# Moving the last 24 modulation column tiles of a diffusion trunk step: from the weight ring to residual places and to the second feed-forward half-step

## The chip, the cores and the metric

The kernel runs on one core of one Trainium2 chip. A core has a matrix engine (TensorE, PE in the profile), a vector engine (VectorE, DVE), a scalar engine (ScalarE, ACT), a general-purpose engine (GpSimd, POOL), and a synchronisation engine (SyncE, SP) that here only issues DMAs. GpSimd issues DMAs too, from a queue of its own. The metric is the time of one execution on the device in microseconds (us). It is judged by the median of several runs.

## The reference

One layer of a diffusion trunk on 640 tokens (512 latent tokens and 128 context tokens) of width 1024, in float32. What matters for the change are the nine modulation vectors, which come from a product of a conditioning vector with a wide matrix, and the places in the layer where each of them is used:

```python
def adaln(cvec, w, b):
    m = jax.nn.silu(cvec) @ w + b
    return m.reshape(cvec.shape[0], N_MOD, D_MODEL)

def layer(x, mods, l, p, ctx):
    m = [mods[:, j][:, None, :] for j in range(N_MOD)]
    g = p['g_norm'][l]
    hh = rmsnorm(x, g[0]) * (1 + m[1]) + m[0]
    x = x + 0.5 * m[2] * swiglu(hh, p['ffn1_w1'][l], p['ffn1_w3'][l], p['ffn1_w2'][l])
    hh = rmsnorm(x, g[1]) * (1 + m[4]) + m[3]
    y, ctx_out = token_mixer(hh, p, l, ctx)
    x = x + m[5] * y
    hh = rmsnorm(x, g[2]) * (1 + m[7]) + m[6]
    x = x + 0.5 * m[8] * swiglu(hh, p['ffn2_w1'][l], p['ffn2_w3'][l], p['ffn2_w2'][l])
    return x, ctx_out
```

The token mixer has a matrix-memory branch (a chunkwise recurrence with a 256 x 256 state for each of four heads) and a differential-attention branch. Each branch has an output product (`w_br_m`, `w_br_d`) whose result is multiplied with a sigmoid gate; the sum of the two goes through `w_out`.

## The kernel before

Features lie on the 128 partitions, eight tiles of them (`KT`), and tokens on the free axis, in two halves of 320 (`HALF`). Products with float32 precision are three matmuls: the weight is split into a high and a low part (`wH`, `wL`; ScalarE copies the high part, VectorE subtracts it), and so is the activation (`hH`, `hL`).

The stages follow one another: the first half-step, the projections and the attention, the matrix-memory stage, the end of the attention branch (product with `w_brd`, evacuated by VectorE as `y1`), the memory branch (product with `w_brm`, evacuated as `ym` and split into `hH` and `hL`), the output product (`w_out`), and the second half-step. TensorE's instructions run in the order in which they are written. Most of the others are put in an order by a scheduler, which looks at their dependencies and an estimate of durations; each engine and each DMA queue then runs its list in order.

*Column tiles.* The modulation of the latent and context tokens needs, for `j` from 2 to 8, 56 tiles of 128 output columns. A tile is a DMA of 128 x 1024 float32 (512 KB, `raw_a<-in_w_ada_c`) and, on VectorE, two reductions of it with the two conditioning rows (`csil`). `Columns.place(n, csil, load, ahead)` says where the next `n` tiles have their buffers and starts to fetch `ahead` of them; `Columns.tile()` takes one: it issues its two reductions and then the next fetch. Behind the eighth tile of a `j` comes a small addition of the bias, and for some of them what uses it (`columns.then`): the scale of the third norm behind `j` = 7, the half gate `half_m[:, 1]` of the last residual addition behind `j` = 8. The first 32 tiles are done in the first half-step. The last 24, of `j` = 6, 7 and 8, are the subject.

*The weight ring.* `rawp` has two slots of 128 x 2048 float32, and all projection weights (`raw<-...`), the re-read attention output (`a_raw`) and the re-read memory output (`z_raw`) go through it, by SP's queue, in order. The last 24 tiles use it as well (`load_columns_raw`, by SP; the reductions write their elementwise product into the other half of the same slot, as bfloat16). Ten of them stand between the cells of the matrix-memory stage, three beside `mem[3].finish`, five beside the last units of the attention branch, and six beside the units of the memory branch, one for every two units.

*Fill.* Products are handed out in units (`Fill`): a granule is the weight of 256 output columns, and has four units of 24 matmuls (two column tiles, two token halves). `fill.slot` runs units between the cells of the matrix-memory stage, `fill.units(2)` and `fill.drain()` run the rest.

*The second half-step.* `HalfStep.run` calls `products` with 20 work items `i` (w1 for even `i`, w3 for odd). An item is seven products of half-size blocks, and for its weights VectorE splits sums of blocks (`ww`, `wC`, `wB`) and evacuates (`s`, `t`, `SO`). `between(i, at)` is called at two places of each item; `hs.at_vec` is the last evacuation on VectorE. The tiles of x (`x_pairs`, in the four places `k0` to `k3`) hold first the layer's input for the residual addition behind `w_out`, then take part in the sums of the activation (`operand_sums`), and are read again from DRAM (`x2_dram`) for the last residual addition. In the kernel before, this re-read is issued at `(0, 1)`.

Of the kernel before, what the change touches and what calls it, by code (L numbers as in the profile page):

```python
# [16 lines left out]
D = 1024  # L17
# [5 lines left out]
KT = D // 128  # L23
# [8 lines left out]
def tile_trunk(ctx: ExitStack, tc: tile.TileContext, a: dict):  # L32
    nc = tc.nc
# [98 lines left out]
    half_m = cp.tile([128, 2, KT, 2], F32, name="half_m")  # L132
# [8 lines left out]
    def half(hf):  # L141
        return slice(hf * HALF, (hf + 1) * HALF)
# [310 lines left out]
    class HalfStep(Winograd):  # L453
# [95 lines left out]
        def run_whole(self, x, gate, final, between, ahead):  # L549
# [47 lines left out]
            for j in range(1, 4):  # L597
                for f in range(2):
                    unit(G[-1], j, f, 1)

        def run(self, x, gate, final, ahead, after):


            def nothing(*args):
                pass

            n = self.n_plain
            down = [Whole(n, self.fetch_w2(0, n, j)) for j in range(4)]

            up = self.ops  # L610
            at = [[up[i] for i in (A11, S1, S2, A12)], [up[i] for i in (S3, S4, A22)], None]

            def fetch(q, i, eng=nc.sync):
                b0, b1 = ((0, n), *GROUPS)[q]
                eng.dma_start(out=at[q][i][:, :, : b1 - b0].bitcast(F32), in_=self.g_dram[i, :, :, b0:b1, :])

            work = self.up_work()
            work[-1][3] = lambda i: {A11: lambda: fetch(0, 0), S1: lambda: fetch(0, 1), S2: lambda: fetch(0, 2), A12: lambda: fetch(0, 3)}.get(i, nothing)()

            def between(i, at):  # L620
                if (i, at) == (0, 1):
                    with tc.issue_after(work[1][0].split_at):
                        after()

            self.products(work, between, down[:2], ahead)
            at[1] += [self.fp.tile([128, 2, 4, HALF], F32R, tag=tag, name="op") for tag in ("gA", "SO")] + at[0][:2]
            x = x()

            def down_done(q, j):
                def done(f, hf, p, u):  # L630
                    d = 2 * j + f
                    if u is not None:
                        p = self.add(p, u)
                    add_residual(x, p, d, hf, gate)
                    if q == 2:
                        final(d, hf)

                def used(i):
                    if q == 1 and j == 3 and i in moves:
                        fetch(2, moves[i], nc.gpsimd)  # L640

                return done, used

            last = [
                [Granule(b1 - b0, self.fetch_w2(b0, b1, j)), lambda i, q=q: at[q][i], *down_done(q, j)]
                for q, (b0, b1) in zip((1, 2), GROUPS) for j in range(4)
            ]
            at[2] = at[0][2:] + at[1][:5]

            moves = {A11: S2, S1: A12, S2: S3, A12: A22, S3: S4}  # L650
            for j in range(4):
                ahead = down[j + 2] if j < 2 else last[j - 2][0]
                loaded = ahead.load()
                with tc.issue_after(loaded):
                    for i in ((A11, S1), (S2, A12), (S3,), ())[j]:
                        fetch(1, i)
                if j < 3:
                    down[j + 1].split()
                else:
                    last[0][0].parts(self.fp)  # L660
                    last[0][0].sums()
                for hf in range(2):
                    for f in range(2):
                        p = acc_tile(self.psum)
                        for kh in range(2):
                            op = at[0][PLAIN_Q[kh, hf]]
                            for b in range(n):
                                w = [down[j].w(i, n * kh + b, f) for i in range(2)]
                                mm3(p, *w, op[:, 0, b], op[:, 1, b], kh + b == 0, kh == 1 and b == n - 1)
                        add_residual(x, p, 2 * j + f, hf, gate)  # L670
                    if (j, hf) == (3, 0):
                        for i in (A22, S4):
                            fetch(1, i, nc.gpsimd)

            def load_last(load=last[3][0].load):
                with tc.issue_after(load()):
                    for i in (A11, S1):
                        fetch(2, i)

            last[3][0].load = load_last  # L680
            self.products(last, nothing, prepared=True)


    csil_dram = dp.tile([2, D], F32, name="csil_dram")
# [45 lines left out]
    x_dram = dp.tile([128, KT, T], F32, name="x_dram")  # L730
    hh2 = []
    stats = []
    with ExitStack() as ph:
# [9 lines left out]
        hs = HalfStep(1, fp, ntmp, psum, a["w1a"], a["w3a"], a["w2a"], FB)  # L743
# [205 lines left out]
        for f, hf in ((0, 1), (1, 1), (0, 0), (1, 0)):  # L949
            p = acc_tile(psum)  # L950
# [3 lines left out]
        with tc.issue_after(end.ins), tc.issue_after(at_act.ins):  # L954
            third, fourth = hs.operand_sums(lambda r: x_all[:, 2 * r : 2 * r + 2, :])
# [5 lines left out]
        columns = Columns(56)  # L961
# [97 lines left out]
        x = Now()  # L1059
# [141 lines left out]
    fill = Fill()  # L1201
# [349 lines left out]
    def pair(tag, i, name):  # L1551
        return in_pools[tag].tile([128, 2, T], F32, tag=f"{tag}{i}", name=name)

    def pairs(tag, name):
        return [pair(tag, i, name) for i in range(4)]
# [138 lines left out]
    with tc.issue_after(box["normed"]):  # L1694
        third, fourth = G.operand_sums(lambda r: box["x"][1][:, 2 * r : 2 * r + 2, :])
# [73 lines left out]
    def aside(hd, qi, part):  # L1769
        if hd == 0:  # L1770
            for _ in range(ROWS.get((qi, part), 0)):
                next(rows, None)
        if part == 0:
            with written():
                fill.low()
        if part == 1 and hd == 1 and qi in (1, 2):
            gate_load(qi - 1)
        if part == 0 and hd == 1 and qi in (2, 3):
            gate_cols()
# [9 lines left out]
    for hd in range(8):  # L1789
        H = heads[hd]  # L1790
        odd = hd % 2
        for qi in range(5):
            n = UNITS[hd][qi]
# [24 lines left out]
        n = UNITS[hd][-1]  # L1818
# [187 lines left out]
    csil2 = ada_p.tile([128, 2, D], F32, name="csil")  # L2006
    dma(csil2, csil_dram.partition_broadcast(128))
    in_order[0] = False
    columns.place(24, csil2, load_columns_raw, 1)
    with written():  # L2010
        fill.units(2)
    for i in range(5):
# [50 lines left out]
    for i in range(5):  # L2063
        fill.one()
        mem[3].finish(i)
        if i > 1:
            columns.tile()
    for k in range(6):
        if k % 3 == 0:
            raw = load(rawp, [128, 3, T], zT_dram[:, k : k + 3, :], tag="raw", name="z_raw")  # L2070
        act(zH[:, k], raw[:, k % 3], AF.Copy)
        tt(vec, zL[:, k], raw[:, k % 3], zH[:, k].bitcast(F32), ALU.subtract)
    while fill.q:
        fill.units(2)
        if columns.n > 6:
            columns.tile()
    ml.close()
    mix.close()

# [1 line left out]
    tmp = ctx.enter_context(tc.tile_pool(name="tmp", bufs=1))  # L2081
    out = ExitStack()
    zp = out.enter_context(tc.tile_pool(name="yy", bufs=1))
    x_pairs = pairs("k", "x")
    x = [x_pairs[d // 2][:, d % 2, :] for d in range(KT)]
    with tc.tile_pool(name="gate", bufs=1) as gp:
        yH, yL = hh_tiles(zp)
        yHL = [(yH[:, k], yL[:, k]) for k in range(KT)]

        def m_evac(g):  # L2090
            def f(p, mt, hf):
                cs = half(hf)
                t = gp.tile([128, HALF], F32, tag="ym", name="ym", bufs=3)
                tt(vec, t, p, gate_of(gm_dram, g, mt, hf, pool=gp, tag="sig", bufs=2), ALU.mult)
                tt(vec, t, t, y1[g][:, mt, cs], ALU.add)
                d = 2 * g + mt
                act(yH[:, d, cs], t, AF.Copy)
                tt(vec, yL[:, d, cs], t, yH[:, d, cs].bitcast(F32), ALU.subtract)
            return f

        for g in range(4):
            fill.granule(a["w_brm"][g], feat_units(psum, m_evac(g), zHL))
        for g in range(4):
            nc.sync.dma_start(out=x_pairs[g], in_=x_dram[:, 2 * g : 2 * g + 2, :])
        while fill.q:
            fill.units(2)
            if columns.n:
                columns.tile()
    ada.close()
    fp = out.enter_context(tc.tile_pool(name="out", bufs=1))  # L2110
    class Halves:
        def __init__(self, lo, hi):
# [9 lines left out]
    raw = load_raw(a["w_out"][3])  # L2122
    t = [in_pools["q"].tile([128, 1024], F32R, tag=f"q{i}", name="wo") for i in range(4)]
# [8 lines left out]
    hs = HalfStep(2, None, tmp, psum, a["w1b"], a["w3b"], a["w2b"], GROUPS[0][0])  # L2132
    st = [Stats(x, hf, tmp) for hf in range(2)]
    x2_dram = dp.tile([128, KT, T], F32, name="x2_dram")
# [60 lines left out]
    third, fourth = hs.operand_sums(lambda r: x_pairs[r])  # L2195
    SO = hs.SO

    def after():
        fourth()
        for g in range(4):  # L2200
            nc.sync.dma_start(out=x_pairs[g], in_=x2_dram[:, 2 * g : 2 * g + 2, :])
        hs.store_g(SO, 0)

    hs.run(
        lambda: x, half_m[:, 1], lambda d, hf: nc.sync.dma_start(out=a["y"][:, d, half(hf)], in_=x[d][:, half(hf)]),
        third, after,
    )


# [126 lines left out]
```

## Time and profile before

| what | us |
|---|---|
| median of 3 runs | 1838.76 (1837.59 to 1839.71) |
| the profiled execution | 1840.36 |
| its span | 1838.6 |
| TensorE busy | 1799.5 |
| VectorE busy | 1317.2 |
| ScalarE busy | 867.7 |

The span is the time from the first to the last instruction of the profiled execution. Busy times are unions over the span, so the rest of TensorE's share is time in which it ran no matmul. A row of a timeline has the start, the duration, the engine, the line of the kernel, the operation, what it writes and reads with the shapes, and in brackets the idle time of the engine before it and what ended it. A row of the waits has the sum in us, the number and the longest. SPq and POOLq are the engines' DMA queues.

### The profile page before, as it was taken

What the parts mean: (1) busy time and instruction counts of PE and PEld (TensorE: products, weight loads), DVE (VectorE), ACT (ScalarE), POOL (GpSimd) and SP (SyncE); (2) the same over time, 40 slices, a digit from 0 to 9 for tenths busy, and PEclk for the clock granted to TensorE, in tenths of its full rate; (3) what the DMA queues carried; (4) which work ended last, traced back from release to release, by engine and by line L of the source; (5) the groups of instructions that cost most, each with busy time, mean ns of one, the idle gap of its engine ahead of it and who ended that gap; (6) DMA issues with size and microseconds to landing.
All of it is one profiled execution on the core that took longest, in us unless ns stands there. A gap on an engine that the chain in (4) does not pass through costs nothing.

```text
span 1838.6 us, 30679 instructions
## 1 busy us (share of the span) xinstructions
PE 1799.5 (98%) x12608; PEld 1761.4 (96%) x12608; DVE 1317.2 (72%) x2148; ACT 867.7 (47%) x1490; POOL 31.0 (2%) x55
## 2 busy tenths in 40 slices
PE   7999999999999999999999999999899999999999
PEld 5999999999999999999999999999899999999999
DVE  5898886577787757475585558876766878887575
ACT  4654454112655555454465555673235645554232
POOL 0000001110000000000000000000000000000000
PEclk8999999999999999999999999999999999999999
DMA  7354547975234322122222154574742345447872
GB/s 289 121 192 169 193 169 250 370 239 176 72 122 145 122 81 79 63 85 67 77 77 84 41 168 147 199 268 164 257 174 86 132 149 188 166 170 254 322 286 87
DMA packets 127709, 298.77 MB, mean 162 GB/s; under 512 B 9617, under 2 KB 90769, under 8 KB 114769
## 3 DMA queue, kind: packets, MB, share of 16 engines
q1 hardware_dynamic: 118306, 256.44, 40.1%
q0 software_dynamic: 9264, 40.37, 6.0%
q8 instruction: 99, 1.62, 0.4%
q14 instruction: 40, 0.33, 0.1%
HBM read 233.15 MB, written 63.63 MB: 161 GB/s over the span
## 4 chain that ended last, share of the span: by engine, by line
PE 84%; DVE 6%; DMA 5%; ACT 3%; issue 1%; SPq 0%; DVEq 0%; ACTq 0%
PE ps_f L75 45%; PE ps_p L75 16%; PE ps_t L75 11%; PE sc L75 3%; PE ps_o L75 2%; PE ps_n L75 2%; DMA ada<-csil_dram 2%; DVE ww L54 1%; PE ps_u L75 1%; PE ps_wT L78 1%; DMA raw_a<-in_w_ada_c 1%; PE ps_qkT L78 1%; DVE raw_a L716 1%; ACT wH L51 1%; PE ps_ss L75 1%
## 5 line engine op out<-in xcount | busy, mean ns | idle before, releaser
L75 PE MATMUL ps_f<-S,ww 128*128 128x320 f32 x2172 | 350.2, 310 | 5.8 <-DVE ww L54 4.2
L75 PEld LDWEIGHTS ps_f<-S,ww 128*128 128x128 f32 x2172 | 327.0, 189 | 8.5 <-DVE ww L54 6.9
L75 PE MATMUL ps_p<-hH,wH 128*128 128x320 f32 x672 | 213.4, 318 | 6.9 <-DVE y L54 6.2
L75 PE MATMUL ps_p<-hL,wH 128*128 128x320 f32 x672 | 208.2, 310 | 0.0
L75 PE MATMUL ps_p<-hH,wL 128*128 128x320 f32 x672 | 208.2, 310 | 0.0
L51 ACT ACTIVATE ww<-raw 128x2048 fp32r<-128x2048 f32 (+1 forms) x67 | 125.6, 1874 | 154.9 <-PE ps_f L75 87.6
L75 PE MATMUL ps_f<-hm,ww 128*128 128x320 f32 x1236 | 195.6, 311 | 2.5 <-DVE ww L54 2.5
L75 PEld LDWEIGHTS ps_f<-hm,ww 128*128 128x128 f32 x1236 | 185.8, 189 | 2.8 <-DVE ww L54 2.8
L75 PE MATMUL ps_t<-wH,hH 128*128 128x256 f32 x640 | 185.3, 289 | 0.9 <-DVE x L57 0.9
L75 PE MATMUL ps_t<-wH,hL 128*128 128x256 f32 x640 | 181.1, 283 | 0.9 <-DVE hL L54 0.9
L75 PE MATMUL ps_t<-wL,hH 128*128 128x256 f32 x640 | 180.9, 283 | 0.0
L54 DVE TENSOR_TENSOR ww<-raw,ww 128x2048 fp32r<-128x2048 f32 (+1 forms) x67 | 150.1, 2240 | 38.7 <-ACT ww L51 38.7
L75 PE MATMUL ps_f<-hm,wB 128*128 128x320 f32 x984 | 157.6, 309 | 0.0
L75 PEld LDWEIGHTS ps_f<-hm,wB 128*128 128x128 f32 x984 | 147.7, 188 | 0.0
L54 DVE TENSOR_TENSOR raw<-raw 128x1024 f32<-128x1024 f32 x159 | 137.6, 865 | 2.0
L75 PEld LDWEIGHTS ps_p<-hH,wH 128*128 128x128 f32 x672 | 126.9, 189 | 7.6 <-ACT wH L51 6.4
L75 PEld LDWEIGHTS ps_p<-hL,wH 128*128 128x128 f32 x672 | 126.9, 189 | 0.3
L75 PEld LDWEIGHTS ps_p<-hH,wL 128*128 128x128 f32 x672 | 126.7, 189 | 0.0
L54 DVE TENSOR_TENSOR wL<-raw,wH 128x2048 fp32r<-128x2048 f32 x43 | 98.3, 2286 | 35.6 <-ACT wH L51 35.6
L75 PEld LDWEIGHTS ps_t<-wH,hH 128*128 128x128 f32 x640 | 122.4, 191 | 1.5 <-ACT nsq L51 1.1
L75 PEld LDWEIGHTS ps_t<-wH,hL 128*128 128x128 f32 x640 | 122.4, 191 | 1.1 <-DVE hL L54 1.1
L75 PEld LDWEIGHTS ps_t<-wL,hH 128*128 128x128 f32 x640 | 122.5, 191 | 0.4
(303 smaller groups left out, 3353.7 us busy)
## 6 DMA issues: line engine op xcount, KB each, us to landing
g_dram<-g SPq DMA_DIRECT2D x44, 640.0 KB, 5.6
raw_a<-in_w_ada_c SPq DMA_DIRECT2D x24, 512.0 KB, 4.0
raw<-in_w1b SPq DMA_DIRECT2D x11, 1024.0 KB, 4.8
raw<-in_w3b SPq DMA_DIRECT2D x11, 1024.0 KB, 4.8
raw<-in_w1a SPq DMA_DIRECT2D x10, 1024.0 KB, 4.8
raw<-in_w3a SPq DMA_DIRECT2D x10, 1024.0 KB, 6.2
ada<-in_w_ada_c POOLq DMA_DIRECT2D x18, 512.0 KB, 5.0
hm<-g_dram POOLq DMA_DIRECT2D x7, 1280.0 KB, 10.5
```

The lines of the kernel that those rows point to most:

```text
L51: return placed(nc.scalar.activation(*args, **kw))
L54: return placed(eng.tensor_tensor(out=out, in0=in0, in1=in1, op=op))
L75: tc.keep_in_program_order(nc.tensor.matmul(*args, **kw))
L78: tc.keep_in_program_order(nc.tensor.transpose(*args, **kw))
L716: placed(vec.tensor_tensor_reduce(out=junk, in0=raw, in1=self.csil[:, v, :], op0=ALU.mult, op1=ALU.add, scale=1.0, scalar=0.0, accum_out=m ...
```

## The change

The 24 tiles are given other places in time and other buffers:

- ten stay in the matrix-memory stage, in the weight ring, as before;
- none is left in the attention branch's end (eight before);
- six stay beside the memory branch's units, but fetched by GpSimd's queue into one buffer of their own (place `k2`), with their product written to `k3` as float32. So only two of the four x loads stand at the beginning of this branch, and the other two follow behind the sixth tile;
- eight stand in the second half-step, at the odd items 3 to 17, with one buffer in `k2`, their product in `k3` and the two `csil` rows read again into `k0` and `k1` at `(1, 1)`. The re-read of x comes at `(18, 1)`, when those places are free again.

```diff
--- before.py
+++ after.py
@@ -598,7 +598,7 @@
                 for f in range(2):
                     unit(G[-1], j, f, 1)
 
-        def run(self, x, gate, final, ahead, after):
+        def run(self, x, gate, final, ahead, aside):
 
 
             def nothing(*args):
@@ -620,7 +620,9 @@
             def between(i, at):
                 if (i, at) == (0, 1):
                     with tc.issue_after(work[1][0].split_at):
-                        after()
+                        aside(i, at)
+                else:
+                    aside(i, at)
 
             self.products(work, between, down[:2], ahead)
             at[1] += [self.fp.tile([128, 2, 4, HALF], F32R, tag=tag, name="op") for tag in ("gA", "SO")] + at[0][:2]
@@ -2006,7 +2008,7 @@
     csil2 = ada_p.tile([128, 2, D], F32, name="csil")
     dma(csil2, csil_dram.partition_broadcast(128))
     in_order[0] = False
-    columns.place(24, csil2, load_columns_raw, 1)
+    columns.place(10, csil2, load_columns_raw, 1)
     with written():
         fill.units(2)
     for i in range(5):
@@ -2063,17 +2065,12 @@
     for i in range(5):
         fill.one()
         mem[3].finish(i)
-        if i > 1:
-            columns.tile()
     for k in range(6):
         if k % 3 == 0:
             raw = load(rawp, [128, 3, T], zT_dram[:, k : k + 3, :], tag="raw", name="z_raw")
         act(zH[:, k], raw[:, k % 3], AF.Copy)
         tt(vec, zL[:, k], raw[:, k % 3], zH[:, k].bitcast(F32), ALU.subtract)
-    while fill.q:
-        fill.units(2)
-        if columns.n > 6:
-            columns.tile()
+    fill.drain()
     ml.close()
     mix.close()
 
@@ -2081,8 +2078,15 @@
     tmp = ctx.enter_context(tc.tile_pool(name="tmp", bufs=1))
     out = ExitStack()
     zp = out.enter_context(tc.tile_pool(name="yy", bufs=1))
-    x_pairs = pairs("k", "x")
-    x = [x_pairs[d // 2][:, d % 2, :] for d in range(KT)]
+    x_pairs = [pair("k", i, "x") for i in range(2)]
+
+    def load_columns_pair(src):
+        raw = pair("k", 2, "raw_a").rearrange("p a t -> p (a t)")[:, :D]
+        nc.gpsimd.dma_start(out=raw, in_=src)
+        return raw, junk
+
+    junk = pair("k", 3, "junk").rearrange("p a t -> p (a t)")[:, :D]
+    columns.place(6, csil2, load_columns_pair, 1)
     with tc.tile_pool(name="gate", bufs=1) as gp:
         yH, yL = hh_tiles(zp)
         yHL = [(yH[:, k], yL[:, k]) for k in range(KT)]
@@ -2100,13 +2104,18 @@
 
         for g in range(4):
             fill.granule(a["w_brm"][g], feat_units(psum, m_evac(g), zHL))
-        for g in range(4):
+        for g in range(2):
             nc.sync.dma_start(out=x_pairs[g], in_=x_dram[:, 2 * g : 2 * g + 2, :])
         while fill.q:
             fill.units(2)
             if columns.n:
                 columns.tile()
+                if not columns.n:
+                    x_pairs += [pair("k", i, "x") for i in range(2, 4)]
+                    for g in range(2, 4):
+                        nc.sync.dma_start(out=x_pairs[g], in_=x_dram[:, 2 * g : 2 * g + 2, :])
     ada.close()
+    x = [x_pairs[d // 2][:, d % 2, :] for d in range(KT)]
     fp = out.enter_context(tc.tile_pool(name="out", bufs=1))
     class Halves:
         def __init__(self, lo, hi):
@@ -2195,15 +2204,36 @@
     third, fourth = hs.operand_sums(lambda r: x_pairs[r])
     SO = hs.SO
 
-    def after():
-        fourth()
-        for g in range(4):
-            nc.sync.dma_start(out=x_pairs[g], in_=x2_dram[:, 2 * g : 2 * g + 2, :])
-        hs.store_g(SO, 0)
+    places = []
+
+    def load_columns_pair(src):
+        raw = pair("k", 2, "raw_a").rearrange("p a t -> p (a t)")[:, :D]
+        nc.gpsimd.dma_start(out=raw, in_=src)
+        return raw, places[2]
+
+    def aside(i, at):
+        if (i, at) == (0, 1):
+            fourth()
+            hs.store_g(SO, 0)
+        elif (i, at) == (1, 1):
+            places.extend(pair("k", j, n).rearrange("p a t -> p (a t)")[:, :D] for j, n in ((0, "csil"), (1, "csil"), (3, "junk")))
+            for v in range(2):
+                nc.sync.dma_start(out=places[v], in_=csil_dram[v].partition_broadcast(128))
+            columns.place(8, Two(places[:2]), load_columns_pair, 1)
+        elif at and 3 <= i < 3 + 15 and i % 2 == 1:
+            columns.tile(hs.at_vec)
+        elif (i, at) == (18, 1):
+            x_pairs[:] = pairs("k", "x")
+            for g in range(4):
+                nc.sync.dma_start(out=x_pairs[g], in_=x2_dram[:, 2 * g : 2 * g + 2, :])
+
+    def residual_pairs():
+        x[:] = [x_pairs[d // 2][:, d % 2, :] for d in range(KT)]
+        return x
 
     hs.run(
-        lambda: x, half_m[:, 1], lambda d, hf: nc.sync.dma_start(out=a["y"][:, d, half(hf)], in_=x[d][:, half(hf)]),
-        third, after,
+        residual_pairs, half_m[:, 1], lambda d, hf: nc.sync.dma_start(out=a["y"][:, d, half(hf)], in_=x[d][:, half(hf)]),
+        third, aside,
     )
```

The order of the other engines moves with it. The first place is SP's queue at the end of the attention branch: `raw<-in_w_brd` and `raw<-in_w_brm` are the ring's weights of the two branches, `raw_a` the tiles, `x` the residual, `sig` the gates. Before:

```order
L97 DMA raw_a<-in_w_ada_c 128x1024
L97 DMA raw<-in_w_brd 128x2048
L97 DMA raw_a<-in_w_ada_c 128x1024 x4
L97 DMA raw<-in_w_brm 128x2048 x2
L2104 DMA x<-x_dram 128x1280 x4
L97 DMA raw_a<-in_w_ada_c 128x1024
L97 DMA sig<-gm_dram 128x1280 x2
```

And after:

```order
L97 DMA z_raw<-zT_dram 128x1920 x2
L97 DMA sig<-gd_dram 128x1280
L97 DMA raw<-in_w_brd 128x2048
L97 DMA raw<-in_w_brm 128x2048 x3
L2108 DMA x<-x_dram 128x1280 x2
L97 DMA sig<-gm_dram 128x1280 x2
L97 DMA raw<-in_w_brm 128x2048
```

The tiles are gone from this queue, and the memory branch's weights stand directly behind the attention branch's last one.

The second place is ScalarE at the end of the matrix-memory stage, behind one and the same evacuation `hs`. `aHL` is the high part of the attention output, `wv`, `Cn`, `num` and `hjunk` belong to the cells, `stage` evacuates a unit of a projection. Before:

```order
L51 ACTIVATE wv<-va,cols 128x258
L51 ACTIVATE Cn<-ps_u 128x258 x2
L51 ACTIVATE hjunk,hss<-hs 128x256 x4
L51 ACTIVATE stage<-ps_p 128x320
L51 ACTIVATE num<-ps_n_12691,cols 128x258
L51 ACTIVATE hjunk,hss<-hs 128x256
L51 ACTIVATE wv<-va,cols 128x258
L51 ACTIVATE rt<-rv 128x5
L51 ACTIVATE ry<-rt 128x5
L51 ACTIVATE num<-ps_n_12713,cols 128x258
L51 ACTIVATE hs<-num,den 128x256
L51 ACTIVATE wv<-va,cols 128x258
```

And after:

```order
L51 ACTIVATE aHL<-a_raw 128x640 x3
L51 ACTIVATE wv<-va,cols 128x258
L51 ACTIVATE hjunk,hss<-hs 128x256
L51 ACTIVATE Cn<-ps_u 128x258 x2
L51 ACTIVATE hjunk,hss<-hs 128x256
L51 ACTIVATE stage<-ps_p 128x320
L51 ACTIVATE hjunk,hss<-hs 128x256 x2
L51 ACTIVATE num<-ps_n_12689,cols 128x258
L51 ACTIVATE hjunk,hss<-hs 128x256
L51 ACTIVATE wv<-va,cols 128x258
L51 ACTIVATE aHL<-a_raw 128x640 x3
```

Before, the first `aHL` copies follow behind the last of these rows; after, three stand ahead of them and three more ahead of the next cells' `num`.

The third place is VectorE in the second half-step, around the low part of a weight block (`ww`) of an odd item. Before:

```order
L54 TENSOR_TENSOR s<-ps_f,u 128x320
L54 TENSOR_TENSOR ww<-raw,ww 128x2048
L54 TENSOR_TENSOR wC<-raw,wC 128x512
L54 TENSOR_TENSOR SO<-ps_f,s 128x320
L54 TENSOR_TENSOR wB<-raw,wB 128x1024
L54 TENSOR_TENSOR t<-ps_f,u 128x320
```

And after, at the third to the eighth tile (at the first two, `ww` and `wC` still stand ahead of `SO`):

```order
L54 TENSOR_TENSOR s<-ps_f,u 128x320
L54 TENSOR_TENSOR SO<-ps_f,s 128x320
L718 ISA junk,mod<-raw_a,csil 128x1024
L718 ISA mod 128x1
L54 TENSOR_TENSOR ww<-raw,ww 128x2048
L54 TENSOR_TENSOR wC<-raw,wC 128x512
L718 ISA junk,mod<-raw_a,csil 128x1024
L718 ISA mod 128x1
L54 TENSOR_TENSOR wB<-raw,wB 128x1024
L54 TENSOR_TENSOR t<-ps_f,u 128x320
```

`SO` and the tile's first reduction moved ahead of `ww`, and the second reduction ahead of `wB`.

## The prediction

> **What bounds the kernel now.** I read the page's shares of busy time and its chain first, since they say whether a stage is worth anything at all.
>
> ```profile
> PE 1799.5 (98%) x12608; PEld 1761.4 (96%) x12608; DVE 1317.2 (72%) x2148; ACT 867.7 (47%) x1490; POOL 31.0 (2%) x55
> PE 84%; DVE 6%; DMA 5%; ACT 3%; issue 1%; SPq 0%; DVEq 0%; ACTq 0%
> ```
>
> TensorE is busy 98% of the span, and its instructions are the same after the change. So only what TensorE loses between matmuls can be won, and every new wait of TensorE adds to the end. The second view is the busy time in stretches around the places that the change empties and fills (columns: window, PE, PEld, DVE, ACT, POOL busy, PE clock, DMA share, GB/s).
>
> ```profile
> 1270.00:1285.00 15.00, 13.92 (x95) 13.66 (x94) 7.59 (x14) 1.92 (x1) 0.00 (x0) 1.00 0.49 172
> 1285.00:1300.00 15.00, 9.71 (x67) 9.45 (x65) 10.36 (x17) 3.25 (x2) 0.00 (x0) 0.91 0.66 236
> 1300.00:1340.00 40.00, 39.10 (x257) 39.13 (x258) 29.35 (x49) 13.03 (x15) 0.00 (x0) 0.95 0.65 230
> 1470.00:1700.00 230.00, 229.17 (x1562) 229.17 (x1563) 183.91 (x232) 116.70 (x159) 0.00 (x0) 1.00 0.52 184
> ```
>
> The end of the attention branch and its border to the memory branch (1270 to 1300) lose over 6 us. The second half-step (1470 to 1700) loses under 1 us of 230, while VectorE has 46 us free there. The third view, the waits from 1220 to 1302, names the loss.
>
> ```profile
> ACT wH L51 <- DMA raw<-in_w_brm: 19.3, 2, 18.7
> ...
> PE ps_p L75 <- DVE y L54: 6.2, 1, 6.2
> ...
> PE ps_p L75 <- DVE wL L54: 1.1, 1, 1.1
> ```
>
> The fourth, the timeline, shows how it comes about: first the queue of SP, then the engines.
>
> ```profile
> 1270.85 16.96 SPq L97 DMA_DIRECT2D raw_a<-in_w_ada_c  x4
> 1290.17 3.94 SPq L97 DMA_DIRECT2D raw<-in_w_brm  x2
> ...
> 1294.40 0.31 PE L75 MATMUL ps_p<-aHL,wL 128*128 128x320 f32 x1
> 1296.12 1.91 ACT L51 ACTIVATE wH<-raw 128x2048 fp32r<-128x2048 f32 x1 [18.70 <-DMA raw<-in_w_brm]
> 1298.06 2.29 DVE L54 TENSOR_TENSOR wL<-raw,wH 128x2048 fp32r<-128x2048 f32 x1 [3.50 <-ACT wH L51]
> 1300.27 0.48 DVE L54 TENSOR_TENSOR y<-ps_p,sig 128x320 f32<-128x320 f32 x1
> 1300.90 0.60 PE L75 MATMUL ps_p<-hH,wH 128*128 128x320 f32 x1 [6.19 <-DVE y L54]
> ```
>
> The four column tiles occupy the weight ring from 1270.85 on, and the memory branch's first weights leave only at 1290.17. Their split (wH, then wL) runs until 1300.35, the last evacuation y is queued behind wL on VectorE, and TensorE, which needs that y for its PSUM, stands for 6.19 us.
>
> **Part 1, the tiles taken out of the attention branch.** No tile is left between 1220 and 1300, and SP then issues the last attention weights and three of the memory branch directly behind one another. What remains at the border is the evacuation alone: TensorE ends at 1294.71 (1294.40 + 0.31), and from the start of y to TensorE's start pass 0.63 (1300.27 to 1300.90). So the gap shrinks from 6.19 to about 0.7, a gain of 5.5, and the other, 1.1 <- wL, goes whole. The gap has a sequel:
>
> ```profile
> 1301.00:1304.00 3.00, 3.00 (x12) 3.00 (x13) 1.95 (x1) 0.00 (x0) 0.00 (x0) 0.50 1.01 418
> 1304.00:1307.00 3.00, 3.00 (x22) 3.00 (x22) 0.22 (x1) 0.00 (x0) 0.00 (x0) 1.00 1.01 339
> ...
> 355.11 3.04 PE L75 MATMUL ps_f<-hm,ww 128*128 128x320 f32 x10 [2.51 <-DVE ww L54]
> ```
>
> Behind it TensorE does 12 matmuls in 3 us where the next 3 us hold 22. Ten matmuls at 3.00/22 = 0.14 are 1.4 to 1.5 us more, and they go too, since a wait of 1.1 or 0.7 leaves no such trace here. Gain 5.5 + 1.1 + 1.5 = 8.1, with 0.1 for the first matmul behind the second gap **8.2**; bounds 7 and 9. The wait of 2.51 us at 352.60 was also followed by slow matmuls (10 in 3.04). [...]
>
> **Part 2, the end of the matrix-memory stage.** A tile's fetch stood between the last projection weights and the first load of the attention output (a_raw). With it gone a_raw takes its slot, and ScalarE's order now has the three copies aHL<-a_raw directly behind hs, ahead of wv, Cn, stage and num, which TensorE needs.
>
> ```profile
> 1188.13 0.33 SPq L97 DMA_DIRECT2D raw_a<-in_w_ada_c  x1
> ...
> 1195.38 0.44 SPq L97 DMA_DIRECT2D a_raw<-aT_dram  x1
> ...
> 1191.66 0.48 ACT L51 ACTIVATE hs<-ps_n,den 128x256 f32<-128x256 f32 x1 [0.38 <-DVE den L1945]
> ...
> 1193.82 0.66 ACT L51 ACTIVATE Cn<-ps_u 128x258 f32<-128x258 f32 x2 [1.22 <-DMA out_new_c<-Cn]
> ...
> 1196.86 0.48 ACT L51 ACTIVATE num<-ps_n,cols 128x258 f32<-128x258 f32 x1
> ...
> 1202.14 2.00 ACT L51 ACTIVATE aHL<-a_raw 128x640 fp32r<-128x640 f32 x3 [1.73 <-DMA a_raw<-aT_dram]
> ...
> 1199.51 0.50 PE L75 MATMUL ps_p<-hH,wH 128*128 128x320 f32 x1
> ```
>
> Before, a_raw was issued at 1195.38 and there at 1202.14, 6.8 us later. Issued at 1188.13 in a quieter stretch, it should be there between 1193.2 (5.1 us, an estimate below that row) and 1194.9 (6.8). ScalarE stands from 1192.1 until then; copies (2.0) and what lies between hs and num (1192.1 to 1197.3, of which Cn waited 1.2, so 4.0) put num's end at landing + 6.0 = 1199.2 to 1200.9, and the matmul group at 1199.51 waits for num. It starts 0 to 1.5 us late. A second block of copies (2.0) stands ahead of the next cells' num, so the next group waits for its num once more; part of that falls into the delay that TensorE has by then, and I allow half of it, 0.3 to 1.0. Sum 0.3 to 2.5, taken **1.8** (1.1 and 0.7); with the slow clock behind one long wait, up to 4.0.
>
> **Part 3, eight tiles in the second half-step.** VectorE splits a weight block (ww) for every item. Where the tile is in the order decides. For the first two of the eight it stands behind ww; for the other six the order is SO, first reduction, ww. SO must wait for TensorE, so ww is later by far than before, where it started 1.15 us ahead of the matmul group of 1541.04 (call that start T).
>
> ```profile
> 1539.89 2.28 DVE L54 TENSOR_TENSOR ww<-raw,ww 128x2048 fp32r<-128x2048 f32 x1
> ...
> 1541.04 1.92 PE L75 MATMUL ps_f<-S,ww 128*128 128x320 f32 x12
> ...
> 1544.56 1.63 PE L75 MATMUL ps_f<-S,ww 128*128 128x320 f32 x10
> ...
> 206.00 1.22 DVE L716 CUSTOM_DVE_ANT_0 junk<-raw_a,csil 128x1024 bf16<-128x1024 f32 x1
> ...
> 208.41 2.28 DVE L54 TENSOR_TENSOR ww<-raw,ww 128x2048 fp32r<-128x2048 f32 x1
> ...
> 219.56 0.49 DVE L54 TENSOR_TENSOR SO<-ps_f,s 128x320 f32<-128x320 f32 x1 [1.27 <-PE ps_f L75]
> 219.97 2.28 DVE L54 TENSOR_TENSOR ww<-raw,ww 128x2048 fp32r<-128x2048 f32 x1
> ...
> 219.36 1.92 PE L75 MATMUL ps_f<-S,ww 128*128 128x320 f32 x12
> ...
> 209.67 0.46 PE L75 MATMUL ps_f<-S,ww 128*128 128x320 f32 x2
> 210.75 1.73 PE L75 MATMUL ps_f<-S,ww 128*128 128x320 f32 x10 [0.62 <-DVE ww L54]
> ```
>
> The first half-step has both pieces. A group that starts at T = 219.36 lets SO start at T + 0.20, and ww follows 0.41 later. In the other, two reductions ahead of ww (2.41 from 206.00 to 208.41, so 1.2 for one) stopped TensorE after two matmuls of the group at T + 3.52; the third, which needs the low half of ww, was due 0.29 into the group, at T + 3.81. For the six tiles ww then ends at T + 0.20 + 0.41 + 1.15 + 2.28 = T + 4.04, and TensorE resumes 0.06 behind (210.69 to 210.75): 0.3 late and 0.1 on its first matmul. Six times 0.39 is **2.3**. Bounds: 0, if one step is 0.3 shorter; 5.3, if each costs what the one at 210 did (210.75 - 209.96 + 0.1 = 0.89). The 8 x 2.4 us of reductions themselves lie in VectorE's free 46.
>
> **Part 4, six tiles beside the memory branch.** They now have one buffer, fetched by GpSimd's queue, and the next fetch leaves only behind the second reduction.
>
> ```profile
> raw_a<-in_w_ada_c SPq DMA_DIRECT2D x24, 512.0 KB, 4.0
> ...
> raw_a<-in_w_ada_c POOLq DMA_DIRECT2D x14, 512.0 KB, 5.3
> ```
>
> A tile takes 5.3 + 2.4 + 0.4 for an evacuation between = 8.1, more than two units of TensorE (2 x 3.52 by the 24 matmuls from 1541.04 to 1544.56 = 7.04). Counted from the branch's first matmul (T0), the second tile ends at about 14 (behind the third unit, 10.6), the sixth at 14 + 4 x 8.1 = 46. The output projection starts at 16 x 3.52 = 56.3 and needs by about 59 a split (2.3) and three evacuations (1.1 each) that stand behind the sixth tile, so it may end at 53. The 7 us cover it: **0.2** for small shifts, and nothing is won. Above 5.3 + 7/4 = 7 us a fetch it begins to cost.
>
> **Part 5, what else moves.** SP issues csil again at the second item and the four x loads at item 18 instead of item 0; both have a whole item or more until they are read, and the x loads no longer compete at the border. **0**, bounds -0.3 and 1.
>
> **The sum.** -8.2 + 1.8 + 2.3 + 0.2 + 0 = -3.9. The profiled execution took 1840.36 (span 1838.6 and 1.8 around it), 1.6 above the median; it would come to 1836.5, the median 1838.76 to **1834.9**. A measurement can tell 0.2%, 3.7 us, from no change.
>
> **The rivals.**
> - Only the ring is freed. Parts 2 and 3 cost 0.4 together: -8.2 + 0.4 + 0.2, 1831.2. For it: in the first half-step most tiles cost TensorE nothing. Against: both orders put the waiting instruction ahead. Chance 0.20, faster.
> - The single buffer sets the pace, slower than before. The six fetches on GpSimd's queue share the DMA with the x loads, gates and weights (share 1.01 at 1301). At 8.5 us each the sixth tile ends at 46 + 4 x 3.2 = 59, 6 us too late, with the slow clock 7.5; with 2 for the same fetches late in the second half-step: -3.9 + 9.5, 1844.4. The gain is gone from 7.7 us a fetch on. [...] The trace has 14 fetches from GpSimd at 5.3, against 4.0 from SP, and none near 8.5 as a median. Chance 0.17, mostly slower.
> - The border's gap stays, since its y finds another late release: only the 1.1 and little else is won, 1838.8 - 1.2 + 4.3 = 1841.9, within the bound. Against it: y itself waits for nothing but its place. Chance 0.05.
> - Parts 2 and 3 at their upper ends, 4.0 and 5.3: -8.2 + 9.5 = 1.3 more than before, 1840.1. Chance 0.15, a quarter of it beyond 1842.4.
> - The forecast, 1833 to 1837: chance 0.43, a little over half of it below 1835.1.
>
> **The numbers.** Faster 0.20 + 0.24 = 0.44; slower 0.15 + 0.04 = 0.19; the same 0.37. The range goes from part 1's gain alone, 1830.5, to 1842, and leaves out most of the second rival and the tail of the fourth. The forecast's own range is 1833 to 1837.
>
> **What would show it.** In the changed profile: no wait over 1 us at the border and no slow matmuls behind it; a wait of 1 to 2 us of ps_p for num near 1200; six waits of 0.3 us for ww in the second half-step, none in its first two tiles; the sixth tile ended 10 us ahead of the output projection. The forecast is wrong if VectorE waits for raw_a beside the memory branch until the output projection, if the wait near 1200 exceeds 3 us, or if ww waits are absent or 0.8 each.

## The result and the profile after

The changed kernel takes 1833.35 us (median of 16 runs, 1832.22 to 1837.85), the kernel before 1838.84 (16 runs, 1836.37 to 1840.74). The ratio is 0.9973 with a 95% interval of 0.9965 to 0.998: faster by 5.5 us, or 0.3%. The profiled execution has a span of 1831.1 us against 1838.6.

TensorE runs the same 12608 matmuls in the same order in both, so the start of one and the same matmul can be compared between two traces. The difference changes only at a few places:

| stretch (us in the profile before) | changed kernel gains |
|---|---|
| first 33 us (code that both share) | 3.9 |
| 33 to 1088, in several steps of both signs | 0.2 |
| 1088 to 1306, the matrix-memory stage (0.1), the end of the attention branch and its border (8.2) | 8.3 |
| 1306 to 1535 | 0 |
| 1535 to 1670, six tiles of the second half-step | -2.3 |
| 1670 to 1704, end of the products | -2.3 |
| sum | 7.8 |

(The spans differ by 7.5; the changed kernel takes 0.3 longer behind the last matmul.) The change itself accounts for 8.3 - 2.3 - 2.3 = 3.7 of these 7.8 us. The 3.9 us at the start come and go with the run (experiment 1).

The busy times in the stretches that answer to those of before (columns: window, PE, PEld, DVE, ACT, POOL busy, PE clock, DMA share, GB/s) show the loss at the border gone, the full clock behind it, and VectorE 16 us busier in the second half-step (200.07 against 183.91):

```profile
1265.00:1280.00 15.00, 15.00 (x105) 15.00 (x104) 4.79 (x7) 1.92 (x1) 0.00 (x0) 1.00 0.20 71
1280.00:1295.00 15.00, 14.32 (x98) 14.09 (x98) 4.70 (x5) 1.92 (x1) 0.53 (x1) 1.00 0.71 242
1295.00:1335.00 40.00, 40.00 (x275) 40.00 (x274) 31.50 (x58) 15.60 (x18) 2.64 (x5) 1.00 0.54 192
1458.00:1690.00 232.00, 230.91 (x1563) 229.33 (x1564) 200.07 (x267) 114.38 (x159) 3.71 (x7) 1.00 0.60 207
```

SP's queue and TensorE in the timeline after: the first two brm weights are issued long before the border, and of the wait only 0.68 us, for the last evacuation y, are left.

```profile
1265.26 14.43 SPq L97 DMA_DIRECT2D raw<-in_w_brm  x2
...
1289.88 0.38 PE L75 MATMUL ps_p<-hH,wH 128*128 128x320 f32 x1 [0.68 <-DVE y L54]
```

The waits of 1660 to 1710 after name the new loss at the end of the products; before, no such wait is there:

```profile
PEld ps_f L75 <- DMA hm<-g_dram: 2.4, 1, 2.4
PE ps_f L75 <- DMA hm<-g_dram: 2.1, 1, 2.1
```

### The profile page after: what moved, and what is told of

It is laid out like the page before. It is cut to its first block, busy times and chain, and to the rows that moved or that the text cites. A ratio compares the mean times of both kernels' runs of the same rounds, so it can differ in the third digit from the quotient of the medians.

```text
span 1831.1 us, 30689 instructions
## 1 busy us (share of the span) xinstructions
PE 1796.7 (98%) x12608; PEld 1757.2 (96%) x12608; DVE 1315.9 (72%) x2148; ACT 864.9 (47%) x1490; POOL 38.3 (2%) x69
## 4 chain that ended last, share of the span: by engine, by line
PE 87%; DVE 6%; DMA 3%; ACT 2%; issue 1%; SPq 0%; DVEq 0%; ACTq 0%
PE ps_f L75 43%; PE ps_p L75 19%; PE ps_t L75 11%; PE sc L75 3%; PE ps_n L75 2%; PE ps_o L75 2%; DVE ww L54 2%; PE ps_u L75 2%; DMA ada<-csil_dram 2%; PE ps_wT L78 1%; DVE junk L718 1%; PE ps_qkT L78 1%; DMA hm<-g_dram 1%; PE ps_ss L75 1%; PE ps_st L75 0%
## 6 DMA issues: line engine op xcount, KB each, us to landing
hm<-g_dram POOLq DMA_DIRECT2D x7, 1280.0 KB, 10.7
```

## The experiments

**1. Both kernels a second time.** `before_again` and `after_again` are the two kernels unchanged.

> The kernel before, unchanged, profiled a second time. Theory: the 3.9 us by which the changed kernel's profile was ahead after the first 33 us, in code that both share, are chance; a second profile of the same kernel then differs from the first there by something between 0 and 4 us, while the waits of 6.2 and 1.1 us at the border of the two branches come back within 0.2 us. Rival: the start belongs to the change; then the second profile is again 3.9 us behind the changed kernel at its 120th matmul.

> The changed kernel again, beside the one above on the same chip: 1833.4, six waits of 0.3 us for ww, 2.1 us for hm, nothing over 0.7 us at the border. The first 33 us can come out about 4 us longer, as in two of the profiles so far, without anything else changing.

`before_again` took 1839.25 (one run); `after_again` 1833.43 (ratio 0.9974, interval 0.9964 to 0.9985). `before_again` was as fast in the first 33 us as the changed kernel's first profile (0.2 us apart), and `after_again` was 2.2 us slower there than that profile. So the start varies from run to run, and the rival falls. The timelines show what it is: the same eight matmuls, in the first profile of before and in the second.

```profile
27.41 2.48 PE L75 MATMUL ps_f<-hm,wH 128*128 128x320 f32 x8
```

```profile
24.80 1.42 PE L75 MATMUL ps_f<-hm,wH 128*128 128x320 f32 x8
```

The same work takes 1.75 times as long in the first. The granted clock over its row was 0.50; in the changed kernel's first profile the same eight took 1.41 us at 1.00. The border did not come back within 0.2 us, which I had expected: `before_again` lost 2.75 and 5.07 us there, with slow matmuls behind both, and against it the changed kernel gains 10.9 at the border instead of 8.3. `after_again` showed the waits that were expected, 2.05 us for hm and 0.68 at the border, but slow matmuls behind hm cost it 1.5 us more. So the losses of both kernels vary from run to run. That may be why the medians differ by 5.5 and not by 3.7; two profiles of each kernel are too few to show it.

**2. The border alone.** `border_alone` leaves out the eight tiles of the second half-step, sets the half gate that they would give to zero, and reads x again at item 0:

```diff
-            hs.store_g(SO, 0)
-        elif (i, at) == (1, 1):
...
-        elif at and 3 <= i < 3 + 15 and i % 2 == 1:
-            columns.tile(hs.at_vec)
-        elif (i, at) == (18, 1):
             x_pairs[:] = pairs("k", "x")
             for g in range(4):
                 nc.sync.dma_start(out=x_pairs[g], in_=x2_dram[:, 2 * g : 2 * g + 2, :])
+            hs.store_g(SO, 0)
+        elif (i, at) == (1, 1):
+            vec.memset(half_m[:, 1], 0.0)
```

> The changed kernel without the eight tiles of the second half-step (the gate of the last residual addition is zero instead, so that part of the computation is left out), and with x read again at item 0 as before. Theory: only the gain at the border is left, 8.3 us: 1838.8 - 8.3 = 1830.5, no wait for ww over 0.25 us in the second half-step and none for hm at its end. Rival (the second half-step's losses do not come from the tiles and the late reading of x): they stay, 1833.

Measured 1830.09 (4 runs; ratio 0.9946, 0.9929 to 0.9964). In its trace TensorE has no wait over 0.25 us from 1465 to the end. Beside the changed kernel's trace the six steps of 0.38 to 0.39 and the one of 2.3 appear one by one. The theory holds: the border is the gain, the second half-step gives part of it back.

**3. Late x without tiles.** `late_x_no_tiles` is the same but with x read again at item 18.

> As the one before, again without the eight tiles (the gate is zero), but x is read again at item 18 as in the changed kernel. Theory (the wait of 2.1 us for hm at the end of the products comes from the 2.6 MB of x in front of it): the wait stays, 1832.8. Rival (it comes from the tiles, which make VectorE late with g, so that what follows in SP's queue goes late): no wait for hm, 1830.5 as without both.

Measured 1830.76 (4 runs; ratio 0.9951, 0.9931 to 0.997). The theory falls: of 2.1 us only 0.3 is left.

```profile
PEld ps_f L75 <- DMA hm<-g_dram: 0.6, 1, 0.6
PE ps_f L75 <- DMA hm<-g_dram: 0.3, 1, 0.3
```

So the bytes of x alone do not make up the 2.1 us, and the tiles have a part in it.

**4. The tile behind ww.** In `behind_ww` a tile waits for the split of the next item's ww in VectorE's order:

```diff
-                if (i, at) == (0, 1):
-                    with tc.issue_after(work[1][0].split_at):
+                if at and i + 1 < len(work):
+                    with tc.issue_after(work[i + 1][0].split_at):
                         aside(i, at)
```

The same condition also puts the second reading of csil and of x behind such a split.

> The changed kernel with each tile of the second half-step issued behind the split ww of the next item instead of behind the last evacuation. Theory (each of six tiles costs 0.39 us because its first reduction stands ahead of ww): the six steps vanish, 2.3 us, 1833.4 - 2.3 = 1831.1. Rival (VectorE is short of time over the whole item, and the wait only moves to wC, wB or SO): no change, 1833.4.

Measured 1839.96 (11 runs; ratio 1.0009, 0.9998 to 1.0021): 6.6 us slower than the changed kernel, worse than either theory. In the trace the waits for ww cost 9 us against the kernel before, and the wait for hm is 2.47. The odd items' ww are on time, but the next item's ww are not. The waits from 1500 to 1690:

```profile
DVE ww L54 <- ACT ww L51: 16.1, 10, 2.4
...
PEld ps_f L75 <- DVE ww L54: 8.9, 6, 1.9
...
PE ps_f L75 <- DVE ww L54: 7.4, 5, 1.6
```

The second reduction now ran from 1535.23, ahead of the differences raw<-raw of the next weights; ScalarE's ww came later for it, VectorE's ww waited 2.41 us for ScalarE, and TensorE 1.64 for VectorE, four times, and once 0.85.

**5. The tile ahead of s.** `before_s` puts the tile behind the last difference raw<-raw of the next item's weights, into the time in which VectorE waited for TensorE's products:

```diff
-            tt(vec, lo[:, nk:], lo[:, nk:], hi[:, nk:], ALU.subtract)
+            self.parts_at = tt(vec, lo[:, nk:], lo[:, nk:], hi[:, nk:], ALU.subtract)
...
-                    aside(i, at)
+                    aside(i, at, work[i + 1][0].parts_at if i + 1 < len(work) else None)
...
-    def aside(i, at):
+    def aside(i, at, behind=None):
...
-        elif at and 3 <= i < 3 + 15 and i % 2 == 1:
-            columns.tile(hs.at_vec)
+        elif not at and 3 <= i < 3 + 15 and i % 2 == 1:
+            columns.tile(behind)
```

> The changed kernel with each tile of the second half-step behind the differences raw<-raw of the next item's weights and so ahead of the evacuation s, for which VectorE waited 2.9 us for TensorE in the kernel before. Theory (what costs is the place in VectorE's order, not the amount of its work): the six waits for ww vanish and no even item pays for it, 1833.4 - 2.3 = 1831.1; if the wait for hm at the end of the products is also VectorE's lateness, it goes too, 1828.8. Rival (VectorE has no room for eight tiles wherever they stand): waits of 1 us and more as with the tile behind ww, 1837 or more.

Measured 1828.74 (5 runs, 1827.65 to 1833.23; ratio 0.995, 0.9937 to 0.9962), the lowest of all medians. All six steps of 0.39 are gone, and the wait for hm fell from 2.1 to 0.5. The stretch of its second half-step shows VectorE as busy as in the changed kernel:

```profile
1458.00:1690.00 232.00, 231.32 (x1575) 231.06 (x1576) 202.20 (x268) 116.24 (x159) 3.72 (x7) 1.00 0.61 214
```

Its order is what differs. At the fourth of the six items the first reduction has gone ahead of s, the second stands between s and ww, and SO, which has to wait for TensorE, follows behind wC. The group T starts at 1602.34, and ww with it, where it was 1.75 us behind in the changed kernel:

```profile
1600.78 0.49 DVE L54 TENSOR_TENSOR s<-ps_f,u 128x320 f32<-128x320 f32 x1 [1.12 <-PE ps_f L75]
1601.19 1.22 DVE L718 CUSTOM_DVE_ANT_0 junk<-raw_a,csil 128x1024 f32<-128x1024 f32 x1
...
1602.33 2.29 DVE L54 TENSOR_TENSOR ww<-raw,ww 128x2048 fp32r<-128x2048 f32 x1
...
1605.14 0.48 DVE L54 TENSOR_TENSOR SO<-ps_f,s 128x320 f32<-128x320 f32 x1
```

So a reduction directly ahead of ww costs nothing here. What cost 0.39 us was SO and a reduction together ahead of ww.

**6. x earlier, with both orders.** `x_earlier` is the changed kernel and `before_s_x16` the kernel of experiment 5, each with the eighth tile at item 4 and x at item 16 (the first line has `not at` in the second of them):

```diff
-        elif at and 3 <= i < 3 + 15 and i % 2 == 1:
+        elif at and i in (3, 4, 5, 7, 9, 11, 13, 15):
...
-        elif (i, at) == (18, 1):
+        elif (i, at) == (16, 1):
```

> The changed kernel with tiles at items 3, 4, 5, 7 to 15, in the same place of VectorE's order as in the changed kernel, and x read again at item 16. If the wait for hm is the bytes of x: gone, 1833.4 - 2.3 = 1831.1. If it is the tiles' lateness or the place of the weights in SP's queue: about 2 us stay, 1833. The waits for ww stay at 0.3 us for the late tiles in both.

> As the one before, with the eighth tile at item 4 and so all of them done by item 15, and x read again at item 16, in a stretch where the DMA has room. If the wait for hm at the end (2.1 us) comes from the bytes of x in front of it: it goes, 1828.8. If it comes from the place of the third and fourth down-projection weights behind the stores of g in SP's queue, which this kernel keeps: it stays, 1831.1. The two tiles at items 3 and 4 follow each other at half the distance; a fetch of 5 us fits 12.3 us.

Measured 1832.93 (10 runs; 0.9971, 0.9962 to 0.998) and 1831.7 (6 runs; 0.9964, 0.9952 to 0.9976). The wait for hm was 1.47 and 1.51 us, so moving x away does not cure it; beside experiment 5 it even rose by 1.0. The bytes of x in front of hm are thus not the whole cause, and with x at item 16 the tiles' place makes no difference to the wait.

**7. Down-projection weights first.** `w2_first` forces hm and S behind the second block of these weights in SP's queue (`begun` holds that block's load):

```diff
-            work[-1][3] = lambda i: {A11: lambda: fetch(0, 0), ...}.get(i, nothing)()
+            def used_last(i):
+                if i in (A11, S1, S2, A12):
+                    with tc.issue_after(begun[0]):
+                        fetch(0, (A11, S1, S2, A12).index(i))
```

> The changed kernel with one thing added: the re-reads of hm and S at the end of the products are issued behind the second column block of down-projection weights, so that its two loads (the third and fourth raw<-in_w2b) stand ahead of the first hm in SP's queue, as in the kernel before, and not between it and the second hm. All eight tiles and the late reading of x stay where they are. Theory (the wait for hm is its lead in SP's queue: it lands 12.7 us after its issue everywhere, and was issued 10.7 us ahead of its use instead of 12.3): lead 12.3, wait 0.5 instead of 2.1, 1831.7. Rival (the tiles' load on the DMA and on VectorE makes it late): the wait stays over 1.3, 1833.

Measured 1833.79 (12 runs; 0.9976, 0.9966 to 0.9986). The wait stays at 2.14 us, so the place of these weights alone is not it either. The chains of waits of the changed kernel, of `before_s`, of `w2_first` and of `x_earlier` have one row each for the transfer that is waited for (start, duration):

```profile
1680.15 12.73 DMA hm<-g_dram
```

```profile
1676.02 12.71 DMA hm<-g_dram
```

```profile
1678.12 12.88 DMA hm<-g_dram
```

```profile
1677.86 13.71 DMA hm<-g_dram
```

TensorE came to need it at 1690.82, 1688.30, 1688.90 and 1690.15: 10.7, 12.3, 10.8 and 12.3 us behind the issue. The first three land in 12.7 to 12.9 us and differ in the lead alone. In the kernel before, the same load has this row in SP's queue:

```profile
1688.63 1.72 SPq L615 DMA_DIRECT2D hm<-g_dram  x1
```

It landed in 12.0 us, and TensorE needed it at 1700.76, 12.1 us behind the issue: just in time. So the 2.1 us of the changed kernel are 1.4 to 1.5 of lost lead and 0.7 of a longer transfer. In these traces, one for each kernel, most of the transfers with the late x are the longer ones: 12.0 us in the kernel before, 12.54 in `late_x_no_tiles`, 12.95 in `behind_ww`, but 11.69 in `brm8`, which has the late x too. The lead goes with the tiles: `late_x_no_tiles` and `before_s` have 12.3. In the changed kernel and in `w2_first` VectorE's last g starts 21.4 to 21.5 us ahead of that point, in `before_s` 22.3 and in the kernel before 22.4. SP stores g and issues everything else in order, so it follows; but that g accounts for 0.8 to 0.9 us of the lead alone, and the rest was not traced. `x_earlier` has the lead, but its transfer took 1.0 us longer, and why stays open.

**8. More tiles beside the memory branch.** `brm8` places eight there and six in the second half-step.

```diff
-    columns.place(6, csil2, load_columns_pair, 1)
+    columns.place(8, csil2, load_columns_pair, 1)
...
-            columns.place(8, Two(places[:2]), load_columns_pair, 1)
-        elif at and 3 <= i < 3 + 15 and i % 2 == 1:
+            columns.place(6, Two(places[:2]), load_columns_pair, 1)
+        elif at and 3 <= i < 3 + 11 and i % 2 == 1:
```

> Eight tiles beside the memory branch and six in the second half-step. Theory (one buffer, 8.1 us for a tile): the eighth ends at 46 + 2 x 8.1 = 62 us after the branch's first matmul, where the evacuations that the output projection needs have to begin at 53; the output projection starts 9 us late, and the slow clock adds 1.5, less 0.8 for two tiles fewer in the second half-step: 1833.4 + 9.7 = 1843. Rival (the evacuations catch up, or the tiles go faster): no wait at the output projection, 1832.6.

Measured 1834.59 (8 runs; 0.9983, 0.9971 to 0.9994). The eighth tile ended at 1351.3, 60.9 us behind the branch's first matmul (62 were expected), but TensorE lost only 0.4 us at the output projection, most of it in a wait of 0.3. VectorE's timeline and the waits of 1344 to 1360 show why:

```profile
1348.54 1.22 DVE L718 CUSTOM_DVE_ANT_0 junk<-raw_a,csil 128x1024 f32<-128x1024 f32 x1 [1.15 <-DMA raw_a<-in_w_ada_c]
...
1349.69 0.48 DVE L54 TENSOR_TENSOR hL<-ym,hH 128x320 fp32r<-128x320 f32 x1
1350.10 1.22 DVE L718 CUSTOM_DVE_ANT_0 junk<-raw_a,csil 128x1024 f32<-128x1024 f32 x1
...
PEld ps_p L75 <- DVE hL L54: 0.3, 1, 0.3
```

Of what the first unit of the output projection needs, one hL alone stands behind a reduction of the last tile, the first one; the split of its weights (1337.74) and the other evacuations stand ahead. The pace was right and the price wrong. The medians of this and the changed kernel are 1.2 us apart, which is not clear of the scatter. In the trace the 0.4 and another 1.8 at the end of the products (a wait of 2.38 for hm and slow matmuls behind it) stand against 0.8 won by two tiles fewer in the second half-step, as expected.

## Why the prediction was right, and where it was not

The forecast was 1834.9 with a range of 1830.5 to 1842; measured were 1833.35, and 3.7 us of gain by the traces' steps against 3.9 in the sum. That agreement is luck in part: two mis-sized terms, parts 2 (1.8 too much) and 5 (2.3 too little), nearly cancel. The median moved by 5.5, and the forecast of it by 3.9.

**Part 1 (8.2): 8.3** between the first profiles, 10.9 against the second one of before. The gap at the border is 0.68 where 0.7 was expected. What was not foreseen is that the loss before varies from run to run.

**Part 2 (1.8): under 0.25.** The order is as described, and ScalarE did stand for a_raw, but TensorE hardly noticed. The rows of SP, ScalarE and the waits:

```profile
1184.68 0.33 SPq L97 DMA_DIRECT2D a_raw<-aT_dram  x1
...
1189.56 1.99 ACT L51 ACTIVATE aHL<-a_raw 128x640 fp32r<-128x640 f32 x3 [1.63 <-DMA a_raw<-aT_dram]
...
1194.46 0.46 ACT L51 ACTIVATE num<-ps_n,cols 128x258 f32<-128x258 f32 x1
...
PEld ps_p L75 <- ACT num L51: 0.2, 1, 0.2
```

a_raw was there 4.9 us after its issue, below the 5.1 that I took as the least, but the issue came later than assumed: on the clock of the profile before, in which this stage lies 4.2 us later, the landing falls at 1193.8, inside the 1193.2 to 1194.9 of the forecast. From there num took 5.4 us to its end at 1194.92 where the sum has 6.0, and TensorE came to its group only at 1195.31. So two terms were too large: the way from the landing to num, by 0.6 us, and with it the 1.1 taken out of 0 to 1.5; and the 0.7 for the second block of copies, which waited 0.15 and cost TensorE nothing.

**Part 3 (2.3): 2.3.** Six steps of 0.38 to 0.39. At the fourth of them:

```profile
1603.88 0.49 DVE L54 TENSOR_TENSOR SO<-ps_f,s 128x320 f32<-128x320 f32 x1 [1.27 <-PE ps_f L75]
1604.29 1.22 DVE L718 CUSTOM_DVE_ANT_0 junk<-raw_a,csil 128x1024 f32<-128x1024 f32 x1
...
1605.43 2.29 DVE L54 TENSOR_TENSOR ww<-raw,ww 128x2048 fp32r<-128x2048 f32 x1
...
1603.68 1.92 PE L75 MATMUL ps_f<-S,ww 128*128 128x320 f32 x12
...
1607.20 2.31 PE L75 MATMUL ps_f<-S,ww 128*128 128x320 f32 x12
```

T is 1603.68, ww ends at 1607.72, T + 4.04 as worked out, and the group at T + 3.52 takes 2.31 us instead of 1.92. Experiment 5 shows that the place in the order is the cause: the 16 us of VectorE's work cost nothing there.

**Part 4 (0.2): 0.** The sixth tile ended at 1335.95, 46.1 us after 1289.88, where 46 was expected. That it agrees to 0.1 is luck: the second tile ended at 15.0 instead of 14, and the four behind it took 7.8 each instead of 8.1. The fetches landed about as forecast, with 5.3; first the six beside the memory branch (tile raw_a, 1285 to 1340), then the eight of the second half-step (1440 to 1690):

```profile
DMA to landing us min/median/max: 3.9/5.1/6.7
```

```profile
DMA to landing us min/median/max: 3.9/4.3/6.0
```

The second rival, the single buffer as the pace, did not occur, and experiment 8 shows that its point of decision was wrong, too early by 8 us: I had put a weight split and three evacuations behind the last tile without looking at where they stand. In the second half-step GpSimd's fetches took 4.3 us as the median and 6.0 at most, beside a VectorE that is busy 86% there (200 of 232).

**Part 5 (0, bounds -0.3 and 1): 2.3.** This step failed. It asked when x is needed, and not what else waits in the same queue: hm, 2.1 us late. Nor does part 3 have a term for it; it prices the tiles by ww alone. By experiments 3, 5 and 7 the late x alone costs 0.3 to 0.6, the place of the down-projection weights nothing, and the tiles' place on VectorE 1.6, the difference between the changed kernel and `before_s`, through the shorter lead of hm. But in experiment 6, with x at item 16, both places of the tiles have a wait of 1.5. So what sets this wait is not fully explained.

**Rivals.** The first (parts 2 and 3 cost 0.4, 1831.2) is 2.2 us from the measured time, the forecast 1.6. What it says of part 2 came true, but part 3 cost what the forecast said. The third and fourth did not occur. Of the signs, the wait for num near 1200 is the one that did not come.

## What to carry to other kernels

Work that is moved to an engine with free time can be had for nothing, but its place in the order decides: here the same eight tiles cost 0 around s, where VectorE waited for TensorE, 2.3 us where six of them made ww follow SO and a reduction, and 9 behind the next item's ww. So look in the trace for the instruction with the long wait, put the work directly ahead of it, and see what the move does to the rows behind. And for a load that is moved, ask what is queued behind it, not only when it is read.

## What the runs showed of the hardware

Whether slow matmuls follow a wait depends on more than its length. At the end of the products the wait for hm was 2.10, 2.14 and 2.05 us in the changed kernel, in `w2_first` and in `after_again`. The 3 us behind each, in the same columns as above:

```profile
1693.00:1696.00 3.00, 3.00 (x21) 3.00 (x22) 0.68 (x2) 0.00 (x0) 0.00 (x0) 1.00 1.02 415
```

```profile
1691.10:1694.10 3.00, 3.00 (x11) 3.00 (x12) 0.25 (x1) 0.00 (x0) 0.00 (x0) 0.50 1.02 415
```

```profile
1695.60:1698.60 3.00, 3.00 (x14) 3.00 (x15) 0.68 (x2) 0.00 (x0) 0.00 (x0) 0.61 1.02 415
```

The shortest of the three was followed by a clock of 0.61 and 14 matmuls, the middle one by the full clock and 21. A wait of 2.47 in `behind_ww` had the full clock behind it, one of 2.38 in `brm8` 0.73. The traces show more. In the profile before, behind the first 40 us, the granted clock changes at 95.66, 99.07, 355.07, 358.49, 1297.15 and 1303.98 us: the slow stretches lasted 3.41, 3.41 and 6.83 us, and the distances between these points are multiples of 3.413 us. In the changed kernel's there is one until the last matmul, from 91.18 to 98.00, of 6.83 us. Around the wait of 2.51 us in the profile before:

```profile
351.66:355.07 3.41, 0.94 (x7) 0.68 (x5) 3.41 (x7) 1.91 (x1) 1.19 (x2) 1.00 0.82 230
355.07:358.49 3.42, 3.38 (x13) 3.38 (x14) 3.42 (x9) 0.00 (x0) 1.49 (x3) 0.50 0.72 239
358.49:361.90 3.41, 3.41 (x25) 3.41 (x25) 3.41 (x4) 0.00 (x0) 0.58 (x1) 1.00 1.00 321
```

In `after_again`, from the end of the wait on:

```profile
1695.52:1696.28 0.76, 0.76 (x5) 0.76 (x6) 0.00 (x0) 0.00 (x0) 0.00 (x0) 1.00 1.01 411
1696.28:1699.69 3.41, 3.41 (x15) 3.41 (x14) 0.68 (x2) 0.00 (x0) 0.00 (x0) 0.50 1.01 411
1699.69:1703.10 3.41, 3.41 (x25) 3.41 (x24) 1.05 (x3) 1.49 (x1) 0.00 (x0) 1.00 1.05 383
```

Take these points, in each profile its own, as borders of cells of 3.41 us. Of the waits above, 2.05, about 2.1 and about 1.9 us lay in one cell (`after_again`, `w2_first`, `brm8`; the last two by the clocks of the stretches behind the waits), and the next cell was slow. The 2.10 of the changed kernel was split into 1.21 and 0.89, and no slow cell followed. Where the borders lie around the 2.47 of `behind_ww` is not shown. In the profiles of before and after, from 40 us to the last matmul, the cells at full clock in which TensorE was idle longest had 2.71, 2.47, 2.44 and 2.12 us, and each of the four was followed by a slow one; behind all the others, with 1.51 at most, none came. This is read from the traces; no run was made to test it. So a wait of 2 to 2.5 us cost itself here and, in some runs, 1.5 us more (3.8 us in `after_again` against 2.3 in the changed kernel, at the end of the products).
